# One sweep for the output projection, a gate product by token halves, and a down projection by weight rows

## The chip, the core and the metric

The kernel runs on one core of a Trainium2 chip. The metric is the device time of one execution in microseconds (us); a kernel's time is the median of several runs. TensorE (PE) multiplies, VectorE (DVE), ScalarE (ACT) and GpSimd (POOL) work element by element, SyncE (SP) issues most transfers. Each engine takes its own instructions in order and waits on semaphores. TensorE writes its sums into PSUM, of which the program uses eight banks of 128 x 512 float32.

## What is computed

A layer with two token mixers between two SwiGLU networks, for 1024 + 32 new tokens and 16 leading ones, 1024 channels wide, 2816 hidden channels, in float32:

```python
x = x + 0.5 * swiglu(rmsnorm(x, norm_ffn1), ...)
... # S5 scan on u, mLSTM on xm and z
mixed = concatenate([rmsnorm(y5, out_norm_s5), rmsnorm(ym, out_norm_ml)], axis=-1)
x = x + mixed @ w_out
x = x + 0.5 * swiglu(rmsnorm(x, norm_ffn2), ffn2_gate, ffn2_up, ffn2_down)
y = rmsnorm(x, norm_final)

def swiglu(x, w_gate, w_up, w_down):
    return (jax.nn.silu(x @ w_gate) * (x @ w_up)) @ w_down
```

The change touches the S5 half of `mixed @ w_out` and all that follows it.

## The kernel before

Channels lie on the 128 partitions, tokens along the free axis: x is eight tiles of 128 channels x 1056 tokens. For float32 accuracy each operand of a matmul is split into a high and a low part: ACT copies the value into the high part (`wh`, `vh`, `xh`, `hh`), DVE subtracts it from the value for the low part (`wl`, `vl`, `xl`, `hl`), and each product is three matmuls (high·high, high·low, low·high). `wslot` (L136) loads a 128 x 1024 slice of weights into one of two raw buffers `wr`, and splits it; `unit` makes the 24 matmuls of one output tile (L161). `psg` and `psm` hand out PSUM banks, four each.

**Output projection, S5 half.** Two sweeps over the tokens, half c=0, then c=1 (528 each). A sweep goes over the eight output tiles o in the order 0, 4, 1, 5, 2, 6, 3, 7, and loads and splits its weights anew. For each o two quarters of 264 tokens are multiplied, DVE scales them by the S5 norm `Rb` out of PSUM (L1168), DVE or, for every second o, POOL adds x (L1169), the result goes to DRAM (`x_d`) and, with the gain of the second FFN's norm, back to x. Squares for that norm are made by ACT and summed by DVE and by POOL (L1152). Once o and o-4 are there, the operands of the next stage are made: `sums` forms differences on POOL (L1291), `split` their high and low parts (ACT L1309, DVE L1310).

**Gate and up.** Two hidden tiles f, f+1 at a time, by a Strassen–Winograd scheme (class `Strassen`): seven products A·B of 512 x 256 weights with 512 x 264 tokens in place of eight. `weights` (L1317) forms the seven weight operands, `gemm` (L1352) the products (L1365), the seven token operands B11, B21, T1, T2, B22, T3, T4 stand in SBUF for each half c. For c=1 and T4 they lie in the tiles `xn` of the S5 branch, which the output projection reads. The first pair is done for c=0 (gate, up), then for c=1 with its weights loaded and split again; seven middle pairs interleave both halves; the last two pairs are again done by halves. `rms_half` (L234) makes the norm's factors for one half: the sum over channels by six one-column matmuls (`col`, L244), a reciprocal root in Newton steps on DVE (`rsqrt`, L251 to L257), and `rms_row`, which spreads it over the partitions by matmuls (`R`, L230). The gate goes through the norm, SiLU and the norm again (`silu`), is multiplied with up (`mul`) and written to DRAM as `h_d`.

**Down.** Three token blocks of 288, 384 and 384. `h_load` reads all 22 hidden tiles of a block and splits them, the first block's during the last gate products; then each output o goes through 22 x 3 matmuls into one bank (L395), with three weight slots for each o, and DVE adds the sum to x (L397). x itself comes back from `x_d` by transfers on POOL's queue (`x_back`, L1200) in two parts, since its space holds raw weights until then.

**Final norm.** `Prep` squares, sums and spreads as above; `out` multiplies the rows of a block (POOL L1223 and L1224, DVE L1226) and stores them (L1231). Blocks 0 and 1 are multiplied and stored later, during the following block; the last one is all that stands behind the last matmul.

`later()` and `behind(es)` place instructions, for engines that are not TensorE, behind what has been issued so far in the program; a scheduler sets the rest of the order.

Of the kernel before, what the change touches and what calls it, by code (L numbers as in the profile page):

```python
# [9 lines left out]
F32 = mybir.dt.float32  # L10
# [18 lines left out]
TAIL = (288, 384, 384)  # L29
# [61 lines left out]
class Kern:  # L91
# [141 lines left out]

    def rms_half(self, R, c, W, a, b):  # L234

        nc = self.nc
        c0 = list(range(0, W - P, P)) + [W - P]
        n = len(c0)
        m, y, t = (self.tp.tile([P, 2 * n], F32, tag=tag + "s", name=tag, bufs=1) for tag in ("rm", "ry", "rt"))
        col = self.psm("col")  # L240
        nc.gpsimd.tensor_tensor(a, a, b, op=ALU.add)
        for i in range(2 * n):
            s = W * (i // n) + c0[i % n]
            nc.tensor.matmul(col[:, i:i + 1], lhsT=a[:, s:s + P], rhs=self.ones, start=True, stop=True)  # L244
# [91 lines left out]
    def gate_up(self, st, wg, wu, R, pool, rest, tail):  # L336

# [3 lines left out]
        W = st.W  # L341
        both = [(f, (0, 1)) for f in range(2, NF - 4, 2)]
        ends = [(f, (c,)) for c in range(2) for f in (NF - 4, NF - 2)]
        for f, cs in [(0, (0,)), (0, (1,))] + both + ends:
            if True:
                sil = {(n, c, q): pool.tile([P, W], F32, tag=f"sil{n}{c}{q}", name="sil") for c in cs for q in range(2) for n in range(2)}

                def silu(n, c, q, src):
                    g, r = sil[n, c, q], R[:, (2 * c + q) * W:(2 * c + q + 1) * W]
                    nc.vector.tensor_tensor(g, src, r, op=ALU.mult)  # L350
                    nc.scalar.activation(g, g, AF.Silu)  # L351
                    nc.gpsimd.tensor_tensor(g, g, r, op=ALU.mult)  # L352

                def mul(n, c, q, src):
                    h = sil[n, c, q]
                    nc.vector.tensor_tensor(h, src, h, op=ALU.mult)
                    t0 = (2 * c + q) * W
                    nc.sync.dma_start(self.h_d[f + n, :, t0:t0 + W], h)
# [4 lines left out]
                st.gemm(wu[f], wu[f + 1], cs, lambda n, c, q: pool.tile([P, W], F32, tag=f"u{q}{n * q}{c}", name="u"), mul)  # L363
                if f == 0 and cs == (0,):
                    with self.later():
                        rest()
                if f == NF - 2 and cs == (0,):
                    tail()

    def h_load(self, pool, t0, n, raws):  # L370

        nc, hs = self.nc, []
        for f in range(NF):
            hh, hl = (pool.tile([P, n], F32R, tag=f"{t}{f}", name=t) for t in ("hh", "hl"))
            raw = raws(f)
            nc.sync.dma_start(raw, self.h_d[f, :, t0:t0 + n])
            nc.scalar.activation(hh, raw, AF.Copy)
            nc.vector.tensor_tensor(hl, raw, hh.bitcast(F32), op=ALU.subtract)
            hs.append((hh, hl))
        return hs  # L380

    def down(self, x, wd, pool, load, raws, post):

        nc = self.nc
        for j, (t0, n) in enumerate(post.blks):
            hs = load(j)
            for o in range(8):
                ps = self.psg()
                for i, (f, nf) in enumerate(((0, 8), (8, 7), (15, 7))):
                    w = self.wslot(wd[o, :, f * P:(f + nf) * P], nf * P, pool if i == 1 else None, 1, raws() if j == 0 else None)  # L390
                    for k in range(nf):
                        wh, wl = (t[:, k * P:(k + 1) * P] for t in w)
                        hh, hl = hs[f + k]
                        for m, (l, r) in enumerate(((wh, hh), (wh, hl), (wl, hh))):
                            nc.tensor.matmul(ps[:, :n], lhsT=l, rhs=r, start=f + k + m == 0, stop=f + k == NF - 1 and m == 2)  # L395
                xs = x[o][:, t0:t0 + n]
                nc.vector.scalar_tensor_tensor(xs, ps[:, :n], 0.5, xs, op0=ALU.mult, op1=ALU.add)  # L397
                post.sq(j, o)
            post.fin(j)
# [541 lines left out]
    def run(self):  # L941
# [193 lines left out]
        h0, esg = ExitStack(), ExitStack()  # L1135
# [442 lines left out]
```

## Time and profile before

| | us |
|---|---|
| median of 3 runs | 2499.73 (2498.15 to 2500.45) |
| the profiled execution's own time | 2500.77 |
| its span in the profile | 2499.1 |
| S5 half of the output projection and first products | 1619.1 to 1769.3 |
| gate and up | 1769.3 to 2140.6 |
| last products, down's first block and into its second | 2140.6 to 2308 |
| rest of the down projection | 2308 to 2480 |
| behind the last matmul | 2480 to 2499.1 |

The profile shows one execution; its times are microseconds from the span's start. The stretches are cut by hand, so that TensorE is busy without a gap in two of them, from 1769.3 to 2140.6 and from 2308 to 2480. A busy share of TensorE says nothing of how fast it runs: for that the profile has the granted clock (PEclk), 1.00 being the full 2.4 GHz.

### The profile page before, as it was taken

How to read it: one execution, taken by the hardware profiler on the slowest of the kernel's cores; microseconds unless marked ns; L12 is line 12 of the kernel's file. 1: busy time of each engine (PE TensorE's matmuls, PEld its weight loads, DVE VectorE, ACT ScalarE, POOL GpSimd, SP SyncE). 2: the span in 40 equal slices, each digit the busy share in tenths (PEclk: the TensorE clock that was granted, in tenths of full speed). 3: DMA queues.
4: the chain of work that ended last, by engine and by line, in shares of the span. 5: the costliest groups of instructions: out<-in, count | busy, mean ns of one | idle time of the engine just before them, and what ended most of it. 6: DMA issues, size and time to landing. Idle time of an engine off the chain costs nothing.

```text
span 2499.1 us, 41152 instructions
## 1 busy us (share of the span) xinstructions
PE 2390.3 (96%) x15656; PEld 2321.0 (93%) x15656; DVE 1491.0 (60%) x2901; ACT 883.6 (35%) x1604; POOL 1031.8 (41%) x1828
## 2 busy tenths in 40 slices
PE   8999999999999999999998989998999999889997
PEld 7999999999999978978898989997999999889997
DVE  7446444444344755537878696687765656966543
ACT  5112211111111433234544316655434344545431
POOL 3004787787787322012235170255544343430001
PEclk9999999999999999999999999998999999999998
DMA  4111222232223323332165452142222222457543
GB/s 152 55 52 55 74 76 82 75 107 82 68 76 95 134 61 68 118 106 80 41 204 178 158 161 106 43 148 91 90 88 89 82 74 86 142 182 237 165 144 111
DMA packets 171309, 264.66 MB, mean 106 GB/s; under 512 B 38704, under 2 KB 113472, under 8 KB 171112
## 3 DMA queue, kind: packets, MB, share of 16 engines
q1 hardware_dynamic: 152456, 230.33, 29.9%
q0 software_dynamic: 9808, 27.32, 3.2%
q10 hardware_dynamic: 8848, 4.38, 0.6%
q8 instruction: 123, 2.02, 0.3%
q14 instruction: 74, 0.61, 0.1%
HBM read 203.44 MB, written 62.72 MB: 107 GB/s over the span
## 4 chain that ended last, share of the span: by engine, by line
PE 64%; POOL 12%; DVE 11%; DMA 5%; issue 4%; ACT 3%; SPq 1%; POOLq 0%; ACTq 0%; DVEq 0%
PE psg L161 33%; PE psg L1365 16%; PE psg L395 8%; POOL E L495 3%; POOL et L495 2%; DMA win_d<-wi 2%; DMA hr<-h_d 1%; PE nu L868 1%; POOL wo L495 1%; PE cps L900 1%; POOL lb L495 1%; PE vp L714 1%; DVE A L629 1%; DVE xl L197 1%; DVE wl L154 1%
## 5 line engine op out<-in xcount | busy, mean ns | idle before, releaser
L161 PE MATMUL psg<-xh,wh 128*128 128x358 f32 (+4 forms) x2272 | 429.2, 328 | 9.4 <-ACT xh L196 8.5
L161 PE MATMUL psg<-xl,wh 128*128 128x358 f32 (+4 forms) x2272 | 424.3, 326 | 0.0
L161 PE MATMUL psg<-xh,wl 128*128 128x358 f32 (+4 forms) x2272 | 419.5, 324 | 0.0
L161 PEld LDWEIGHTS psg<-xh,wh 128*128 128x128 f32 x2272 | 372.9, 191 | 19.6 <-ACT xh L196 10.5
L161 PEld LDWEIGHTS psg<-xl,wh 128*128 128x128 f32 x2272 | 374.1, 191 | 5.0 <-issue 4.4
L161 PEld LDWEIGHTS psg<-xh,wl 128*128 128x128 f32 x2272 | 371.4, 190 | 3.8 <-issue 3.3
L153 ACT ACTIVATE wh<-wr 128x1024 fp32r<-128x1024 f32 (+1 forms) x170 | 176.4, 1037 | 403.2 <-PE psg L161 247.3
L154 DVE TENSOR_TENSOR wl<-wr,wh 128x1024 fp32r<-128x1024 f32 (+1 forms) x170 | 211.7, 1245 | 93.1 <-ACT wh L153 82.2
L314 DVE SCALAR_TENSOR_TENSOR x<-psg,x 128x358 f32<-128x358 f32 (+1 forms) x264 | 137.8, 527 | 100.1 <-PE psg L161 99.5
L395 PE MATMUL psg<-hh,wh 128*128 128x384 f32 (+1 forms) x528 | 171.5, 325 | 3.6 <-ACT wh L153 3.6
L395 PE MATMUL psg<-hh,wl 128*128 128x384 f32 (+1 forms) x528 | 171.1, 324 | 2.2 <-DVE wl L154 2.2
L395 PE MATMUL psg<-hl,wh 128*128 128x384 f32 (+1 forms) x528 | 170.4, 323 | 0.0
L161 PE MATMUL psg<-hh,wh 128*128 128x358 f32 (+1 forms) x528 | 133.4, 333 | 1.0 <-DVE x L314 1.0
L352 POOL TENSOR_TENSOR sil<-sil,Ra 128x264 f32<-128x264 f32 x88 | 85.1, 978 | 117.8 <-ACT sil L351 117.8
L161 PE MATMUL psg<-hl,wh 128*128 128x358 f32 (+1 forms) x528 | 131.9, 328 | 0.0
L161 PE MATMUL psg<-hh,wl 128*128 128x358 f32 (+1 forms) x528 | 129.5, 326 | 0.0
L273 DVE TENSOR_TENSOR gt<-psg,Ra 128x358 f32<-128x358 f32 (+1 forms) x66 | 34.8, 529 | 127.7 <-PE psg L161 120.9
L282 DVE TENSOR_TENSOR hf<-sil,psg 128x358 f32<-128x358 f32 (+1 forms) x66 | 34.8, 527 | 124.8 <-PE psg L161 124.8
L1435 POOL TENSOR_TENSOR acc<-acc,sq 128x358 f32<-128x358 f32 (+2 forms) x36 | 38.8, 1077 | 170.0 <-ACT sq L1433 169.3
L395 PEld LDWEIGHTS psg<-hh,wh 128*128 128x128 f32 x528 | 99.2, 188 | 4.8 <-ACT wh L153 4.8
L395 PEld LDWEIGHTS psg<-hh,wl 128*128 128x128 f32 x528 | 99.1, 188 | 2.9 <-DVE wl L154 2.9
L495 POOL TENSOR_TENSOR E<-E,et 128x8 f32<-128x8 f32 (+6 forms) x256 | 97.7, 382 | 3.8
(398 smaller groups left out, 4923.1 us busy)
## 6 DMA issues: line engine op xcount, KB each, us to landing
x<-w2g SPq DMA_DIRECT2D x28, 512.0 KB
x<-w2u SPq DMA_DIRECT2D x28, 512.0 KB
wr<-w2d SPq DMA_DIRECT2D x32, 448.0 KB
wr<-win SPq DMA_DIRECT2D x24, 512.0 KB
wr<-wout SPq DMA_DIRECT2D x24, 512.0 KB
h_d<-sil SPq DMA_DIRECT2D x88, 132.0 KB
wr<-w1g SPq DMA_DIRECT2D x22, 512.0 KB
wr<-w1u SPq DMA_DIRECT2D x22, 512.0 KB
```

What stands on the lines that cost most here:

```text
L153: nc.scalar.activation(vh, r, AF.Copy)
L154: nc.vector.tensor_tensor(vl, r, vh.bitcast(F32), op=ALU.subtract)
L161: self.nc.tensor.matmul(ps[:, :n], lhsT=a[k], rhs=b[k], start=i == 0, stop=i == 3 * nk - 1)
L197: nc.vector.scalar_tensor_tensor(l, s, gain, h.bitcast(F32), op0=ALU.mult, op1=ALU.subtract)
L273: nc.vector.tensor_tensor(gt[:, :n], ps[:, :n], R[:, t0:t0 + n], op=ALU.mult)
L282: nc.vector.tensor_tensor(hf[:, :n], sil[:, :n], ps[:, :n], op=ALU.mult)
L314: nc.vector.scalar_tensor_tensor(xs, ps[:, :n], 0.5, xs, op0=ALU.mult, op1=ALU.add)
L352: nc.gpsimd.tensor_tensor(g, g, r, op=ALU.mult)
L395: nc.tensor.matmul(ps[:, :n], lhsT=l, rhs=r, start=f + k + m == 0, stop=f + k == NF - 1 and m == 2)
L495: PT = lambda o, x, y, op: nc.gpsimd.tensor_tensor(o, x, y, op=op)
L1365: nc.tensor.matmul(ps[c, bank], lhsT=l[:, k * P:(k + 1) * P], rhs=r[k], start=start and i == k == 0, stop=i == 2 and k == 3, skip_group_ch ...
L1435: e.tensor_tensor(d, d, sq, op=ALU.add)
```

## The change

1. The S5 half of the output projection is a single sweep: each weight is loaded and split once and used for four token quarters; the first two output tiles go together. Additions of x and of squares are all DVE's. `early(k)` makes the token operands of c=0 within the sweep; `late(1)` makes the 28 splits and 16 differences of c=1 behind it (L1287 is the split's DVE line now), with `behind(es, 20)`.
2. The first pair's gate product runs all seven steps for c=0 and then for c=1; `rms_quarters` makes the norm's factors of all four quarters between the two, and their rows `R` are spread within the steps of c=1. All eleven pairs do both halves, each weight loaded once.
3. Down has blocks of 360, 360 and 336 tokens. The first two go by hidden tiles f: one row of the weights (`w2f`, 128 x 1024) and one tile of h are loaded and split, and 24 matmuls of 360 columns add to eight banks, one for each output. The third block goes by outputs as before; its h is read during the second block. x comes back in two transfers on POOL's queue behind the last up product. Rows and stores of each block follow its own norm.

The diff's core:

```diff
-        for f, cs in [(0, (0,)), (0, (1,))] + both + ends:
+        us = self.wp.tile([P, 1024], F32, tag="wr", name="u")
+        for f in range(0, NF, 2):
...
-                st.gemm(wg[f], wg[f + 1], cs, lambda n, c, q: sil[n, c, q], silu)
-                if f == 0 and cs == (0,):
-                    st.late(1)
+            st.gemm(wg[f], wg[f + 1], lambda n, c, q: sil[n, c, q], silu, rest if f == 0 else None)
+            st.gemm(wu[f], wu[f + 1], u, mul)
...
+        for j in range(last):
+            t0, n = blks[j]
+            ps = [(self.psg if o % 2 == 0 else self.psm)("psd") for o in range(8)]
+            for f in range(NF):
+                hh, hl = self.h_load(self.hp, f, t0, n, wide, bufs=4)
+                w = self.wslot(wf[f])
+                if j == last - 1:
+                    hs.append(self.h_load(pool(), f, *blks[last], wide, tag=str(f)))
+                for l, rs in zip(w, ((hh, hl), (hh,))):
+                    for o in range(8):
+                        for i, r in enumerate(rs):
+                            nc.tensor.matmul(ps[o][:, :n], lhsT=l[:, o * P:(o + 1) * P], rhs=r, start=f == i == 0 and l is w[0], stop=f == NF - 1 and l is w[1])
             for o in range(8):
...
+                add(j, o, ps[o])
...
             for c in range(2):
...
+            st.early(0)
+            for i, o in enumerate(order[2:], 2):
+                w = load(o)
+                for c in range(2):
+                    ot = new()
+                    for q in (2 * c, 2 * c + 1):
+                        evict(ot, self.unit(w, xn, W2 * q, W2), q)
+                    done(i, o, c, ot)
+                    if c == 0 and i % 2:
+                        st.early(i // 2)
...
         w = self.weights((src1, src2))
-        ps, u = {}, {}
+        if rest is not None:
+            with ExitStack() as es:
+                K.behind(es, 20)
+                self.late(1)
...
+        for i in range(7):
+            step(i, 0)
+        rows = rest()
+        for i in range(7):
+            step(i, 1)
+            if i == 0:
+                rows()
+                for h in held:
+                    out(*h)
```

Up to the output projection the two programs have the same instructions in the same order. Three places behind it follow, each as it stands before and after.

DVE, the reciprocal root of the norm. Before, the second half's (`rm`, `ry`, `rt`) stands in the middle of the first up product for c=1, and its steps come one behind another:

```order
L356 TENSOR_TENSOR sil<-psg,sil 128x264
L1334 TENSOR_TENSOR vl<-Rb,vh 128x512
L245 TENSOR_SCALAR rm<-col 128x6
L253 TENSOR_SCALAR ry<-rm 128x6
L255 TENSOR_TENSOR rt<-ry 128x6
L256 SCALAR_TENSOR_TENSOR rt<-rt,rm 128x6
L257 SCALAR_TENSOR_TENSOR ry<-rt,ry 128x6
```

After, the root of all four quarters (its tiles lie in x) stands among the last of the 28 splits of c=1 (`xl`); L347 is the first use of the factors:

```order
L257 SCALAR_TENSOR_TENSOR x<-x 128x12
L255 TENSOR_TENSOR x<-x 128x12
L1287 TENSOR_TENSOR xl_112<-x,xh_111 128x264
L256 SCALAR_TENSOR_TENSOR x<-x 128x12
L257 SCALAR_TENSOR_TENSOR x<-x 128x12
L1287 TENSOR_TENSOR xl_114<-x,xh_113 128x264
L255 TENSOR_TENSOR x<-x 128x12
L256 SCALAR_TENSOR_TENSOR x<-x 128x12
L1287 TENSOR_TENSOR xl_114<-x,xh_113 128x264
L257 SCALAR_TENSOR_TENSOR x<-x 128x12
L347 TENSOR_TENSOR sil<-sil,Ra 128x264
```

All 28 splits of c=1 now stand ahead of the root's last step (the last L257), the last five of them among the root's steps; before, no split stood between the column's sum and the root.

TensorE, the rows `R` that carry the root to all partitions. Before, they stand right behind `col`, in the middle of the up product for c=1:

```order
L1365 MATMUL psg<-xl_102,vh 128x264 x2
L1365 MATMUL psg<-xh_99,vl 128x264 x2
L1365 MATMUL psg<-xh_101,vl 128x264 x2
L244 MATMUL col<-ones,Ra 128x1 x6
L230 MATMUL R<-ident,ry 128x128 x2
L230 MATMUL R<-ident,ry 128x8
L230 MATMUL R<-ident,ry 128x128 x2
L230 MATMUL R<-ident,ry 128x8
L1365 MATMUL psg<-xh_103,wh 128x264 x2
```

After, three of four stand behind two steps of c=1 (twelve matmuls on B11, twelve on T1), and behind them the rest of the gate product:

```order
L1376 MATMUL psg<-xl_104,vh 128x264 x2
L1376 MATMUL psg<-xl_106,vh 128x264 x2
L1376 MATMUL psg<-xh_103,vl 128x264 x2
L1376 MATMUL psg<-xh_105,vl 128x264 x2
L230 MATMUL R<-ident,x 128x128 x2
L230 MATMUL R<-ident,x 128x8
L230 MATMUL R<-ident,x 128x128 x2
L230 MATMUL R<-ident,x 128x8
L230 MATMUL R<-ident,x 128x128 x2
L230 MATMUL R<-ident,x 128x8
L1376 MATMUL psg<-xh_107,wh 128x264 x2
L1376 MATMUL psg<-xh_109,wh 128x264 x2
```

The splits that the steps of c=1 read (`xh`, `xl`) and the root that `R` reads are made by the same DVE stretch.

SP, from gate and up to down. Before, h's first block is read and weights for down are issued between the last writes of h; `x<-w2d` are raw weights that lie in x's space:

```order
L1324 DMA x<-w2g 128x2x512
L358 DMA h_d<-sil 128x264
L376 DMA x<-h_d 128x288 x2
L358 DMA h_d<-sil 128x264
L376 DMA x<-h_d 128x288 x6
L358 DMA h_d<-sil 128x264
L1324 DMA x<-w2g 128x2x512
L376 DMA x<-h_d 128x288 x6
L152 DMA x<-w2d 128x2x512
```

After, one row of weights goes ahead of the last six writes of h, and reads of h and rows of weights take turns:

```order
L355 DMA h_d<-sil 128x264 x8
L152 DMA wr<-w2f 128x1024
L355 DMA h_d<-sil 128x264 x3
L369 DMA hr<-h_d 128x360 x3
L355 DMA h_d<-sil 128x264 x3
L152 DMA wr<-w2f 128x1024
L369 DMA hr<-h_d 128x360
L152 DMA wr<-w2f 128x1024
L369 DMA hr<-h_d 128x360 x3
L152 DMA wr<-w2f 128x1024
L369 DMA hr<-h_d 128x360 x2
```

The reads of h for the first block moved behind nearly all of its writes, and the weights for down go through the two buffers `wr`.

## Rows read from the trace of the kernel before

**Rows 1.** The page's first line.

```profile
span 2499.1 us, 41152 instructions
```

**Rows 2.** Windows, all engines: window, length, busy of each engine, PEclk, DMA share, GB/s.

```profile
1619.10:1769.30 150.20, 131.09 (x988) 129.74 (x987) 123.74 (x209) 77.72 (x143) 78.91 (x70) 0.90 0.37 119
1769.30:2140.60 371.30, 371.30 (x3038) 371.18 (x3039) 233.06 (x351) 156.17 (x316) 171.10 (x147) 0.99 0.26 84
2140.60:2308.00 167.40, 151.69 (x1117) 147.75 (x1116) 121.17 (x186) 87.08 (x158) 40.55 (x33) 0.99 0.62 193
2308.00:2480.00 172.00, 172.00 (x984) 172.00 (x982) 71.62 (x94) 58.69 (x79) 8.95 (x7) 1.00 0.47 140
2480.00:2499.10 19.10, 6.29 (x41) 5.69 (x41) 7.46 (x23) 2.12 (x4) 6.72 (x7) 0.58 0.46 165
```

**Rows 3.** Windows, PE by line: L161, then L1365, then L395.

```profile
1619.10:1769.30 150.20, 95.28 (x746) 0.90 0.37 119
...
1619.10:1769.30 150.20, 27.65 (x169) 0.90 0.37 119
...
2140.60:2308.00 167.40, 64.54 (x492) 0.99 0.62 193
...
2140.60:2308.00 167.40, 87.49 (x613) 0.99 0.62 193
2308.00:2480.00 172.00, 171.56 (x972) 1.00 0.47 140
```

**Rows 4.** Waits of PE, 1619.1 to 2308: total us, times, longest.

```profile
PE psg L1365 <- ACT vh L1333: 13.2, 3, 9.2
...
PE R L230 <- DVE ry L257: 2.4, 1, 2.4
```

**Rows 5.** DVE groups by shape, 1619.1 to 1769.3: busy, mean ns, idle; then POOL's L1291.

```profile
L1310 DVE TENSOR_TENSOR xl<-x,xh 128x264 fp32r<-128x264 f32 x32 | 21.3, 694 | 5.4 <-ACT xh L1309 5.3
...
L1168 DVE TENSOR_TENSOR ot<-psg,Rb 128x264 f32<-128x264 f32 x32 | 13.6, 425 | 5.4 <-PE psg L161 2.7 <-issue 1.5 <-ACT Rb L231 1.0
...
L1310 DVE TENSOR_TENSOR B22l<-x,B22h 128x264 fp32r<-128x264 f32 x4 | 3.9, 980 | 0.0
...
L1291 POOL TENSOR_TENSOR x<-x x32: 735/761/1184, 1637.9 to 1737.3; 128x264 f32<-128x264 f32 x32
```

**Rows 6.** PE's timeline around 2179.57: start, duration, count, idle before.

```profile
2174.84 0.65 PE L1365 MATMUL psg<-xh,wl 128*128 128x264 f32 x4
2179.57 1.25 PE L1365 MATMUL psg<-xh,vh 128*128 128x264 f32 x4 [4.08 <-ACT sil L1370]
```

**Rows 7.** Groups by shape, 2308 to 2480.

```profile
L154 DVE TENSOR_TENSOR wl<-wr,wh 128x1024 fp32r<-128x1024 f32 x14 | 17.8, 1270 | 34.2 <-ACT wh L153 34.2
...
L378 DVE TENSOR_TENSOR hl<-hr,hh 128x384 fp32r<-128x384 f32 x15 | 8.6, 595 | 11.7 <-ACT hh L377 11.6
L397 DVE SCALAR_TENSOR_TENSOR x<-psg,x 128x384 f32<-128x384 f32 x14 | 7.8, 556 | 17.6 <-PE psg L395 17.6
```

**Rows 8.** ACT's timeline, 2342 to 2349; landing of x_d; a window.

```profile
2342.37 0.96 ACT L153 ACTIVATE wh<-wr 128x896 fp32r<-128x896 f32 x1 [1.09 <-DMA wr<-w2d]
...
2345.95 1.06 ACT L153 ACTIVATE wh<-wr 128x1024 fp32r<-128x1024 f32 x1 [1.57 <-DMA wr<-w2d]
...
DMA to landing us min/median/max: 4.3/5.6/10.4
...
2220.00:2308.00 88.00, 84.95 (x607) 83.20 (x606) 52.19 (x86) 43.16 (x69) 2.29 (x3) 1.00 0.74 232
```

**Rows 9.** Timelines of DVE, POOL and SP at the end.

```profile
2482.81 0.60 DVE L216 TENSOR_SCALAR rm<-col 128x1 f32<-128x1 f32 x3 [2.24 <-PE col L214]
...
2485.22 0.16 DVE L257 SCALAR_TENSOR_TENSOR ry<-rt,ry 128x3 f32<-128x3 f32 x1
...
2485.24 6.72 POOL L1224 TENSOR_TENSOR x<-x,Rb 128x384 f32<-128x384 f32 x7 [48.91 <-ACT Rb L231]
...
2487.23 5.14 SPq L1231 DMA_DIRECT2D o_y<-x  x4
```

More of the change, by code (lines that the diff above doesn't have):

```diff
@@ L333, in ffn, with gate_up @@
                 pass
-    def gate_up(self, st, wg, wu, R, pool, rest, tail):
+    def gate_up(self, st, wg, wu, R, pool, rest):
         nc = self.nc
         self.h_d = self.tc.dram_tile([NF, P, TO], F32, name="h_d")
-        W = st.W
-        both = [(f, (0, 1)) for f in range(2, NF - 4, 2)]
-        ends = [(f, (c,)) for c in range(2) for f in (NF - 4, NF - 2)]
-        for f, cs in [(0, (0,)), (0, (1,))] + both + ends:
[L345 to L358, printed above, removed]
-                st.gemm(wg[f], wg[f + 1], cs, lambda n, c, q: sil[n, c, q], silu)
-                if f == 0 and cs == (0,):
-                    st.late(1)
[L363 to L382, printed above, removed]
-        nc = self.nc
-        for j, (t0, n) in enumerate(post.blks):
-            hs = load(j)
-            for o in range(8):
[L388 to L399, printed above, removed]
@@ new lines, in run, with second @@
+            st.early(0)
[3 more added lines that the diff above has]
+                    ot = new()
+                    for q in (2 * c, 2 * c + 1):
+                        evict(ot, self.unit(w, xn, W2 * q, W2), q)
+                    done(i, o, c, ot)
+                    if c == 0 and i % 2:
+                        st.early(i // 2)
+        gu = esg.enter_context(tc.tile_pool(name="gu", bufs=1, reuse_waits="tile"))
+        def rest():
+            with self.later():
+                rows = self.rms_quarters(Ra, W2)
+            def second():
+                with self.later():
+                    rows()
+            return second
@@ L1202, in run @@
[L1202 to L1217 removed]
+                nc.gpsimd.dma_start(xa[:, k:k + 4, :TO], x_d[k:k + 4].rearrange("k p t -> p k t"))
@@ L1382, in gemm, with emit @@
-        for c in cs:
-            add(nc.vector, u[c, 2], mm(c, "d", "S4", "B22", start=False), u[c, 2])
-            out(0, c, 1, u[c, 2])
-        for c in cs:
-            keep(c, 3, mm(c, "a", "S3", "T3", start=False), new(1, c, 0))
-            add(nc.gpsimd, u[c, 5], u[c, 3], u[c, 5])
-            out(1, c, 1, u[c, 5])
-        for c in cs:
-            out(1, c, 0, mm(c, "a", "A22", "T4", start=False))
+        def emit(n, c, q, t):
+            if rest is not None and c == 0:
+                held.append((n, c, q, t))
+            else:
+                out(n, c, q, t)
@@ new lines, in gemm, with __init__, tile @@
+        if rest is None:
+            for i in range(7):
+                for c in range(2):
+                    step(i, c)
+            return
+        for i in range(7):
+            step(i, 0)
+        rows = rest()
+        for i in range(7):
+            step(i, 1)
+            if i == 0:
+                rows()
+                for h in held:
+                    out(*h)
+class _Spare:
+    ROWS = {"rm": (0,), "ry": (1, 2), "rt": (3,), "rms": (4,), "rys": (5,), "rts": (6,)}
+    def __init__(self, x):
+        self.x, self.i = x, {}
+    def tile(self, shape, dt, tag=None, name=None, bufs=1):
+        r = self.ROWS[tag]
+        i = self.i[tag] = self.i.get(tag, -1) + 1
+        return self.x[:, r[i % len(r)], :shape[1]]
```

314 lines of the change are left out of this document (170 added, 144 removed).

## The prediction

> **What bounds the kernel now.** I cut the span into windows by what TensorE does and divide matmul time by instruction, since the change leaves the number of matmul columns as it is: only the gaps between matmuls can change. The span is 2499.1 us [rows 1], the execution's own time 2500.77, 1.04 above the median of 2499.73; my sum of gains is taken off the median.
>
> From 1769.3 to 2140.6 TensorE never stops: 3038 matmuls of 264 columns in 371.30 us, 0.1222 us each [rows 2]. From 2308 to 2480 it doesn't stop either: 972 of 384 columns take 171.56 us, 0.1765 each [rows 3]. Both are 0.46 ns a column, so a matmul of 360 columns is estimated at 0.1655 us, one of 288 at 0.1328, and the order in which columns are grouped is worth nothing. What can be won lies in three places.
>
> A, 1619.1 to 1769.3 (150.2 us): 746 + 169 matmuls of 264 columns [rows 3] are worth 915 x 0.1222 = 111.8 us. The rest, 38.4 us, is gaps, a clock of 0.90 [rows 2] and the 73 other small matmuls; about 5 us of these small ones (my choice; the norm needs them in any order) stays, so **33 us** are losses. The list of waits shows the largest: 13.2 us on the weight split `vh`, 9.2 in one piece [rows 4].
>
> B, 2140.6 to 2308 (167.4 us): 492 x 0.1222 + 528 x 0.1328 (down's first block) + 85 x 0.1765 = 145.2 us, so **22 us** are losses.
>
> C, behind the last matmul: **19.1 us** [rows 2].
>
> **The change, part by part.**
>
> *Single sweep.* Eight weight loads and splits go; DVE takes over POOL's additions. DVE then has, by the mean durations of [rows 5] and [rows 7], 32 evictions at 0.425, 16 additions and 14 sums of squares of 528 columns at twice that, 26 splits at 0.694 and eight weight splits at 1.27: 13.6 + 13.6 + 11.9 + 18.0 + 10.2 = 67 us in a sweep of 94 us (768 x 0.1222). TensorE's matmuls hide it but for about 2 us (0 to 6) where evictions come late: four of the eight banks serve the sweep, so DVE may lag by some three units of 2.9 us before TensorE waits.
>
> *First gate product.* Time 0 is TensorE's start on it. c=0 takes 84 x 0.1222 = 10.3 us, `col` about 1, the two steps of c=1 ahead of `R` 2.9: TensorE comes to `R` at about 14. `R` waits for the root's last step, which DVE's order has behind all 28 splits. DVE comes to the first split at about 6 (my estimate: two evictions, an addition and squares, and two weight splits are still ahead of it). How long do 28 splits take while POOL makes 16 differences? Undisturbed, a 264-column instruction is 0.425 us (L1168, whose source is PSUM [rows 5]): 11.9 us. The 32 measured `xl` splits beside POOL's differences have a mean of 0.694 [rows 5]: 19.4. If DVE and POOL took strict turns, 11.9 + 16 x 0.761 = 24.1. I take the measured 19.4. The root itself is 2.6 us (2482.81 to 2485.38 [rows 9]). So `R` is ready at 6 + 19.4 + 2.6 = 28, the wait 14 (7 to 19). A wait of 4.08 us let the next four matmuls take 1.25 in place of 0.65 us [rows 6] for some 3 us, so the clock adds about 2: 16 (9 to 21). Behind it the up product starts with its evictions in arrears: 1 (0 to 3). A' = 2 + 16 + 1 = **19** (9 to 30) in place of 33: gain 14.
>
> At this place the Trainium skill, "SBUF — State Buffer", § Who interferes with whom, has a rule against the change: a DVE instruction with two SBUF inputs and a GpSimd instruction that reads SBUF lock each other out for a whole instruction, while one with a single SBUF input goes free. The trace agrees in kind: L1168 (one operand in PSUM) stays at 0.425 while `B22l` takes 0.980, about one split plus half to all of a difference. By the strict rule the splits take the 24.1 us above, A' is 24 and the time about 5 us later than by the row.
>
> *From up to down.* h's first tile can be read when it is written, so what stands between the last up matmul and down is the first splits: `hh` and `hl` of one tile, 0.53 + 0.595 [rows 7] = 1.2 us. One raw weight buffer stays occupied by `u` until the last product: 1. The two reads of x (4.3 MB) run beside the first hidden tiles; reads of a part of it landed in 4.3 to 10.4 us [rows 8], and 232 GB/s was moved with TensorE nearly full in 2220 to 2308 [rows 8]: 1.5 (0 to 4).
>
> *Down by rows.* For each f there are 24 matmuls, 24 x 0.1655 = 3.97 us, and DVE splits 1.27 + 0.56, ACT 1.06 + 0.53: hidden. The second block reads 512 KB of weights and 2 x 172 KB of h in 3.97 us, about 220 GB/s, near the 232 above: 1.5 (0 to 4). Between the blocks all eight banks have to be evicted: 8 x 0.52 (0.556 [rows 7] by 360/384) = 4.2 us; the first bank is finished 1.2 us before the last, and the next block asks for a bank each 0.33 us, for the last at 2.3: 0.7 without and 1.9 with all overlap lost, I take 1.4. Into the third block 0.3. B' = 1.2 + 1 + 1.5 + 1.5 + 1.4 + 0.3 = **7** (2 to 14) in place of 22: gain 15.
>
> *Tail.* POOL's seven rows, 0.96 us each, ended at 2491.96 [rows 9]; four belong to block 1 and now go earlier. `Rb` stays 7.6 behind the last matmul, three rows of 336 columns (0.84) end at 10.2, the last store is issued 0.4 later and the span ended 6.7 after that issue: 17.3, gain **2** (0 to 4).
>
> Sum: 14 + 15 + 2 = 31, and 2499.7 - 31 = **2469 us**.
>
> **Rivals.**
>
> R1, the first gate product waits as long as all that is saved ahead of it. DVE and POOL take strict turns, and the wait is followed by a late up product: A' stays at 33. For it: `R` stands behind every split, and the measured `B22l` of 0.980; against: the mean of 0.694. Time 2499.7 - 17 = 2483.
>
> R2, slower: the raw weight buffers of down. There are two, and a buffer's round is the load's landing L, ACT's copy 1.06, DVE's split 1.27 and about 0.3 of issue; two buffers serve f's of 3.97 us if L + 2.6 is at most 7.9, so L up to 5.3. Before, two copies that both waited for a transfer started 3.58 us apart (2342.37, 2345.95 [rows 8]); two buffers make a round of 7.2 and L about 4.5, while h was read as well. That speaks against it, narrowly; for it speaks that x, h and weights now come together, and that x's own reads took up to 10.4. Each microsecond of L above 5.3 costs half a microsecond for each of 44 f's, 22 us; from L = 6.7 on the gain of 31 is gone, at L = 8 the time is 2528.
>
> R3, TensorE loses its clock while it goes round eight banks. The Trainium skill, "TensorE: Matmul & The Clock Gate", § A second HAM failure mode: psum-queue depth-cycling, tells of a kernel whose clock swung when it cycled banks in each iteration. As a mechanism of this kernel: at half clock the two blocks' 1056 matmuls take 175 us more, 2644. Against it: in 1769.3 to 2140.6 products change banks every twelve matmuls at a clock of 0.99, and no gap is to be seen [rows 2].
>
> R4, all is hidden: splits undisturbed at 11.9 (A' at 9) and B' at 2: gains of 24 + 20 + 4, about 2452.
>
> **How the numbers follow.** Forecast (2457 to 2480) 0.66; R1 0.15; R4 0.10; R2 0.07, of which 0.02 ends within no change; R3 0.02. The likeliest gives 2469. The range 2450 to 2492 takes in the forecast, R1, most of R4 and the mildest of R2, and leaves out about 0.13. A change under 0.2% (5 us) can't be told from none. Faster by more is the forecast, R1 and R4, less 0.01 for mishaps that add up: 0.90; within 0.03; slower 0.07.
>
> **What would show it.** Sweep: TensorE gaps from its start to the first gate matmul under 6 us in all. First gate: one wait of `R` on the root's last `ry` of about 14 us (7 to 19), splits of 0.6 to 0.8 on the mean, PEclk below 1 behind it; a mean near 0.42 speaks for R4, near 0.85 for R1. Up to down: TensorE idle 2 to 4 us. Down: 24 matmuls each 4 us at PEclk 1.00, ACT's copies waiting for TensorE rather than for transfers; waits of TensorE on `wh` or `wl` that come back every f are R2, a PEclk near 0.5 is R3. Tail: 17 us. I am wrong if the losses of A don't lie in the doubled weights and sweeps but in something that the single sweep keeps, or if the first gate's steps wait for something ahead of `R`.

## The result and the profile after

The changed kernel takes **2453.51 us** (median of four runs, 2450.63 to 2458.17) beside 2499.38 on the same chip: ratio 0.9818, 95% interval 0.9801 to 0.9835, 45.9 us less. Measured twice more beside other runs of the kernel before it had 0.9817 (0.9795 to 0.9838) and 0.9810 (0.9796 to 0.9823). The profiled execution took 2452.73, its span is 2451.0 us, 48.1 shorter than [rows 1].

Not all of the 48.1 us belongs to the change. The first row here is TensorE's row `R` ahead of the S5 half of the output projection, the second the `col` of the last norm, right behind the last matmul; both of the kernel before (start, duration, line, idle time before):

```profile
1617.55 1.56 PE L230 MATMUL R<-ident,ry 128*128 128x128 f32 x6 [3.81 <-DVE ry L257]
...
2479.82 3.40 PE L214 MATMUL col<-ones,sqd 128*128 128x1 f32 x30
```

and the same `R` after:

```profile
1613.80 1.43 PE L230 MATMUL R<-ident,ry 128*128 128x128 f32 x6 [3.82 <-DVE ry L257]
```

In front of it the two programs are alike, and yet it starts 3.75 us earlier; in the profiles of this study it starts anywhere from 1608 to 1618 us, whichever kernel it is, so this is no effect of the change (its cause was not looked for). I therefore compare stretches from here on. From this row to the last `col` (2434.97, below) it is 821.2 us in place of 862.3: **41.1 less**; behind it 16.0 in place of 19.3: **3.3 less**.

Windows of the changed kernel, all engines (columns as in [rows 2]): the sweep, the first gate product and into its up product, the rest of gate and up, down's three blocks:

```profile
1615.50:1710.30 94.80, 94.00 (x769) 93.82 (x769) 68.37 (x139) 47.53 (x92) 18.03 (x20) 0.99 0.27 88
1710.30:1757.00 46.70, 40.52 (x290) 39.04 (x289) 39.29 (x71) 25.46 (x63) 26.35 (x29) 0.85 0.19 63
1757.00:2176.00 419.00, 419.00 (x3456) 419.00 (x3455) 251.70 (x391) 170.12 (x348) 187.14 (x164) 1.00 0.27 87
2176.00:2265.00 89.00, 88.27 (x538) 88.06 (x537) 42.22 (x57) 38.60 (x55) 0.03 (x1) 1.00 0.62 207
2265.00:2355.00 90.00, 90.00 (x551) 90.00 (x550) 54.75 (x82) 47.03 (x73) 0.00 (x0) 1.00 0.61 199
2355.00:2435.00 80.00, 80.00 (x529) 80.00 (x527) 39.09 (x65) 29.36 (x40) 12.81 (x11) 1.00 0.51 157
```

From 1757 to 2435 TensorE is busy without a gap but for one at 2176, at a clock of 1.00; the losses of 2140.6 to 2308 in [rows 2] have gone. The sweep is 94.80 us for 768 matmuls whose bare time is 93.8. What is left ahead of the last matmul lies in the second window, at a clock of 0.85. TensorE's waits, from 1600 to the end (total, times, longest; the first row is left out, the two waits at a norm's root that lie outside the change, 3.8 at the `R` shown above and 2.3 behind the last matmul):

```profile
...
PE psg L1376 <- ACT sil L1381: 4.9, 3, 3.0
PE R L230 <- DVE x L257: 2.0, 2, 1.2
PE psd L398 <- ACT hh L370: 0.7, 1, 0.7
```

The 13.2 on `vh` of [rows 4] have no successor. TensorE in the first pair (start, duration, idle before):

```profile
1710.32 0.65 PE L1376 MATMUL psg<-B11h,wh 128*128 128x264 f32 x4
...
1720.83 1.25 PE L1376 MATMUL psg<-T3h,wh 128*128 128x264 f32 x4 [2.96 <-ACT sil L1381]
...
1733.54 1.25 PE L1376 MATMUL psg<-xh,vh 128*128 128x264 f32 x4 [1.47 <-ACT sil L1381]
...
1738.21 2.15 PE L230 MATMUL R<-ident,x 128*128 128x128 f32 x18 [1.24 <-DVE x L257]
```

DVE in the same stretch:

```profile
1717.12 8.62 DVE L1287 TENSOR_TENSOR xl<-x,xh 128x264 fp32r<-128x264 f32 x12
...
1726.01 8.83 DVE L1287 TENSOR_TENSOR xl<-x,xh 128x264 fp32r<-128x264 f32 x11
...
1737.90 0.16 DVE L257 SCALAR_TENSOR_TENSOR x<-x 128x12 f32<-128x12 f32 x1
```

DVE comes to the first split of c=1 6.8 us behind TensorE's start (1717.12 - 1710.32), has made 28 of them when the root's last step starts at 1737.90, and `R` starts 27.9 us behind the product's start. The steps on the way wait now and then for ACT's copies out of PSUM (`sil`), which stand in ACT's queue behind the copies for the splits.

Between up and down, and behind the last matmul:

```profile
2177.14 1.60 PE L398 MATMUL psd<-hh,wh 128*128 128x360 f32 x8 [0.73 <-ACT hh L370]
```

```profile
2434.97 3.40 PE L214 MATMUL col<-ones,sqd 128*128 128x1 f32 x30
...
2442.79 2.60 POOL L1232 TENSOR_TENSOR x<-x,Rb 128x336 f32<-128x336 f32 x3 [45.40 <-ACT Rb L231]
...
2444.56 1.25 SPq L1239 DMA_DIRECT2D o_y<-x  x2
```

One wait of 0.73 us for the first tile of h; and three rows on POOL in place of the seven of [rows 9]. ACT's copies in down (waits from 2176 to 2435) wait for TensorE far more often than for a row of weights:

```profile
ACT wh L153 <- PE psd L398: 45.5, 29, 2.9
...
ACT wh L153 <- DMA wr<-w2f: 5.2, 2, 3.6
```

### The profile page after: what moved, and what is told of

It reads as the page before. It is cut to its first block, busy times and chain, and to the rows that moved or that the text cites. A ratio compares the mean times of both kernels' runs of the same rounds, so it can differ in the third digit from the quotient of the medians.

```text
span 2451.0 us, 40952 instructions
## 1 busy us (share of the span) xinstructions
PE 2372.5 (97%) x15656; PEld 2307.7 (94%) x15656; DVE 1436.2 (59%) x2858; ACT 861.4 (35%) x1576; POOL 972.5 (40%) x1790
## 4 chain that ended last, share of the span: by engine, by line
PE 68%; POOL 11%; DVE 9%; DMA 5%; issue 4%; ACT 2%; SPq 1%; POOLq 0%; ACTq 0%; DVEq 0%
PE psg L161 35%; PE psg L1376 18%; PE psd L398 7%; POOL E L511 3%; POOL et L511 2%; DMA win_d<-wi 1%; PE psg L410 1%; DVE xl L197 1%; PE cps L916 1%; DMA rb<-rb_d 1%; PE nu L884 1%; POOL wo L511 1%; PE vp L730 1%; POOL lb L511 1%; DVE xl L1287 1%
## 5 line engine op out<-in xcount | busy, mean ns | idle before, releaser
L161 PE MATMUL psg<-xh,wh 128*128 128x358 f32 (+4 forms) x2272 | 428.0, 327 | 8.7 <-ACT xh L196 7.9
L161 PE MATMUL psg<-xl,wh 128*128 128x358 f32 (+4 forms) x2272 | 421.8, 325 | 0.0
L161 PE MATMUL psg<-xh,wl 128*128 128x358 f32 (+4 forms) x2272 | 419.2, 324 | 0.0
L161 PEld LDWEIGHTS psg<-xh,wh 128*128 128x128 f32 x2272 | 371.4, 190 | 18.9 <-ACT xh L196 9.7
L161 PEld LDWEIGHTS psg<-xl,wh 128*128 128x128 f32 x2272 | 371.8, 190 | 4.9 <-issue 4.4
L161 PEld LDWEIGHTS psg<-xh,wl 128*128 128x128 f32 x2272 | 371.1, 189 | 3.7 <-issue 3.3
L153 ACT ACTIVATE wh<-wr 128x1024 fp32r<-128x1024 f32 (+1 forms) x182 | 190.9, 1049 | 401.8 <-PE psg L161 266.7
L154 DVE TENSOR_TENSOR wl<-wr,wh 128x1024 fp32r<-128x1024 f32 (+1 forms) x182 | 229.1, 1259 | 121.3 <-ACT wh L153 84.0
L161 PE MATMUL psg<-hh,wh 128*128 128x358 f32 (+1 forms) x528 | 133.7, 334 | 0.9 <-DVE x L314 0.9
L161 PE MATMUL psg<-hl,wh 128*128 128x358 f32 (+1 forms) x528 | 132.1, 329 | 0.0
L161 PE MATMUL psg<-hh,wl 128*128 128x358 f32 (+1 forms) x528 | 129.9, 327 | 0.0
L349 POOL TENSOR_TENSOR sil<-sil,Ra 128x264 f32<-128x264 f32 x88 | 79.1, 914 | 120.6 <-ACT sil L348 120.5
L398 PE MATMUL psd<-hh,wh 128*128 128x360 f32 x352 | 113.8, 327 | 0.7 <-ACT hh L370 0.7
L398 PE MATMUL psd<-hl,wh 128*128 128x360 f32 x352 | 113.8, 327 | 0.0
L1232 POOL TENSOR_TENSOR x<-x,Rb 128x360 f32<-128x360 f32 (+1 forms) x11 | 10.9, 1018 | 245.4 <-ACT Rb L231 245.4
L511 POOL TENSOR_TENSOR et<-E 128x8 f32<-128x8 f32 (+6 forms) x256 | 92.8, 362 | 19.1
L161 PEld LDWEIGHTS psg<-hh,wh 128*128 128x128 f32 x528 | 92.5, 190 | 2.5 <-DVE x L314 2.3
L161 PEld LDWEIGHTS psg<-hl,wh 128*128 128x128 f32 x528 | 94.3, 190 | 0.0
```

Source lines behind the costliest of these rows:

```text
L153: nc.scalar.activation(vh, r, AF.Copy)
L154: nc.vector.tensor_tensor(vl, r, vh.bitcast(F32), op=ALU.subtract)
L161: self.nc.tensor.matmul(ps[:, :n], lhsT=a[k], rhs=b[k], start=i == 0, stop=i == 3 * nk - 1)
L398: nc.tensor.matmul(ps[o][:, :n], lhsT=l[:, o * P:(o + 1) * P], rhs=r, start=f == i == 0 and l is w[0], stop=f == NF - 1 and l is w[1])
L511: PT = lambda o, x, y, op: nc.gpsimd.tensor_tensor(o, x, y, op=op)
```

## The experiments

Twelve runs; times are medians beside the kernel before on the same chip.

| run | us | ratio (95%) |
|---|---|---|
| down alone | 2469.33 | 0.9891 (0.9876 to 0.9905) |
| before, additions on DVE | 2489.95 | 0.9980 (0.9969 to 0.9990) |
| before, POOL out of the sweeps | 2484.26 | 0.9945 (0.9925 to 0.9964) |
| changed, two sweeps | 2453.50 | 0.9823 (0.9808 to 0.9839) |
| changed, one raw buffer | 2540.10 | 1.0176 (1.0157 to 1.0195) |
| changed, weights read twice | 2464.48 | 0.9857 (0.9839 to 0.9876) |
| changed, low parts twice | 2461.18 | 0.9870 (0.9835 to 0.9906) |
| changed, differences on DVE | 2447.35 | 0.9802 (0.9773 to 0.9831) |
| the same again | 2445.87 | 0.9786 (0.9772 to 0.9799) |
| the same, `col` earlier | 2452.87 | 0.9806 (0.9786 to 0.9827) |
| changed, again | 2451.42 | 0.9817 (0.9795 to 0.9838) |
| changed, again | 2452.45 | 0.9810 (0.9796 to 0.9823) |

**How the gain divides.** The kernel before takes over the third part and, of the second, the undivided last two pairs; its two sweeps and its first pair by halves stay:

```diff
-TAIL = (288, 384, 384)
+TAIL = (360, 360, 336)
...
-        both = [(f, (0, 1)) for f in range(2, NF - 4, 2)]
-        ends = [(f, (c,)) for c in range(2) for f in (NF - 4, NF - 2)]
-        for f, cs in [(0, (0,)), (0, (1,))] + both + ends:
+        both = [(f, (0, 1)) for f in range(2, NF, 2)]
+        for f, cs in [(0, (0,)), (0, (1,))] + both:
```

and `h_load`, `down`, `x_back` and `out` as in the change.

> The kernel before with the third part of the change alone: all pairs behind the first interleaved, down by weight rows, x back at once, rows behind each norm; two sweeps and the first pair by halves stay. Theory, the gains of the stages are independent: the stretch from the last products to the last matmul loses some 2 us in place of 22 and the tail 3 less, so 2499.4 - 23 = about 2476 (2472 to 2481). Rival, the gain hangs on the first two parts (for instance because the first products' backlog runs on): less than 10 us, 2490 or more.

Measured: 2469.33, 26 us less than the kernel before. Its `R` and its last `col`, and its largest waits:

```profile
1613.28 1.57 PE L230 MATMUL R<-ident,ry 128*128 128x128 f32 x6 [3.79 <-DVE ry L257]
...
2451.66 3.40 PE L214 MATMUL col<-ones,sqd 128*128 128x1 f32 x30
```

```profile
PE psg L1349 <- ACT vh L1317: 9.2, 1, 9.2
```

From `R` to `col` 838.4 us: 23.9 of the 41.1 come from this part, and by difference 17.2 (838.4 - 821.2) from the sweep and the first pair. This holds to about 1 us: 1.2 of the 23.9 lie ahead of the first pair's `R`, where this program is still the kernel before (from that `R` to the last `col` it is 2451.66 - 1761.16 = 690.5 us in place of 2479.82 - 1766.60 = 713.2, so 22.7 less). The wait of 9.2 us on `vh` of the kernel before stands as it was. The theory of independent stages holds, and this part is larger than the 23 forecast.

**What the sweep's single pass is worth.** The changed kernel's sweep goes over the outputs twice, by halves, with sixteen weight loads:

```diff
-            w = [load(o) for o in order[:2]]
             for c in range(2):
+                w = [load(o) for o in order[:2]]
...
-            st.early(0)
-            for i, o in enumerate(order[2:], 2):
-                w = load(o)
-                for c in range(2):
+                if c == 0:
+                    st.early(0)
+                for i, o in enumerate(order[2:], 2):
+                    w = load(o)
```

> The changed kernel with its sweep cut in two by token halves again: sixteen weight loads and splits in place of eight, all else as changed. Theory, the weights lie under the matmuls and the stage's gain comes from where the splits of c=1 and POOL's work went: within 4 us of the changed kernel's 2453.5 (2450 to 2458), the stretch of the output projection 95 to 97 us. Rival, the halved weight traffic is what the sweep gains: 10 us or more slower, 2463 and up.

Measured: 2453.50, the same. The first gate product starts at 1709.72 behind an `R` at 1613.01, 96.7 us, after the change 96.5 (1710.32 - 1613.80). Halving the weight loads is worth nothing here: what the first part gains comes from where other work went.

**What was lost there before.** In the kernel before, the wait of 9.2 us on `vh` [rows 4] begins on POOL and DVE; POOL, then DVE, then ACT around it:

```profile
1724.01 5.19 POOL L1169 TENSOR_TENSOR ot<-x,ot 128x264 f32<-128x264 f32 x1 [3.31 <-DVE ot L1168]
```

```profile
1723.85 1.79 DVE L1310 TENSOR_TENSOR xl<-x,xh 128x264 fp32r<-128x264 f32 x5
1725.57 1.21 DVE L1334 TENSOR_TENSOR wl<-x,wh 128x1024 fp32r<-128x1024 f32 x1
1726.70 0.76 DVE L1310 TENSOR_TENSOR xl<-x,xh 128x264 fp32r<-128x264 f32 x2
1727.39 1.21 DVE L1334 TENSOR_TENSOR wl<-x,wh 128x1024 fp32r<-128x1024 f32 x1
1730.85 5.36 DVE L1310 TENSOR_TENSOR xl<-x,xh 128x264 fp32r<-128x264 f32 x4 [2.24 <-ACT xh L1309]
```

```profile
1729.23 0.73 ACT L1171 ACTIVATE x<-ot,vec 128x528 f32<-128x528 f32 x1 [4.64 <-POOL ot L1169]
...
1731.66 0.61 ACT L1333 ACTIVATE vh<-x 128x512 fp32r<-128x512 f32 x1
```

One addition of 264 columns takes 5.19 us on POOL (a difference of that size has a median of 0.761 [rows 5]) while DVE runs seven splits and two weight splits with no pause, up to 1728.60; it ends at 1729.20, 0.6 us after they do. ACT waits 4.64 us for it, and `vh` stands in ACT's queue behind that. The first run takes the additions off POOL:

```diff
-                        (nc.gpsimd if i % 2 else nc.vector).tensor_tensor(t, x[o][:, t0:t0 + n], t, op=ALU.add)
+                        nc.vector.tensor_tensor(t, x[o][:, t0:t0 + n], t, op=ALU.add)
...
-                    e, d = (nc.gpsimd, accs[c][1]) if i % 2 else (nc.vector, accs[c][0])
+                    e, d = nc.vector, accs[c][i % 2]
```

> The kernel before with all additions of its two sweeps (x, and the squares) on DVE, none on POOL: a piece of the first part alone. Theory, POOL's slow additions and their fight with DVE make the backlog that TensorE waits 9.2 us for at the first gate product: 8 us or more gained, 2491 or less. Rival, the backlog is DVE's and ACT's own splits in the middle of the sweeps: DVE, busy 124 of 150 us there, takes 14 us more, and the time stays within 5 us of 2499 or grows.

Measured: 5.4 us gained by the medians, 5.0 by the ratio; the theory's 8 did not come, and the rival's number is met or just missed. POOL and TensorE there:

```profile
1714.85 4.51 POOL L1291 TENSOR_TENSOR x<-x 128x264 f32<-128x264 f32 x1 [5.28 <-DVE xl L1310]
...
1724.94 1.25 PE L1365 MATMUL psg<-T1h,vh 128*128 128x264 f32 x4 [11.14 <-ACT vh L1333]
```

The wait has not gone but moved: now a difference (L1291) is starved for 4.51 us behind the same dense run. The second run takes the differences off POOL as well:

```diff
-        sub = lambda o, x, y: self.K.nc.gpsimd.tensor_tensor(o, x, y, op=ALU.subtract)
+        sub = lambda o, x, y: self.K.nc.vector.tensor_tensor(o, x, y, op=ALU.subtract)
```

> As the last but the differences of the token operands too are DVE's: POOL has nothing left of the kernel before's two sweeps but the sums of weights. In the run before this one the wait of TensorE at the first gate product stayed (11.1 us), now behind one difference on POOL that took 4.51 us while DVE ran splits and sums back to back, as an addition had taken 5.19 in the kernel before. Theory, POOL is starved there by DVE's dense run and ACT, TensorE stand behind it: the wait on the split vh falls to 3 us or less and 10 us or more are gained on the kernel before. Rival, DVE's total load sets the wait: 32 more instructions of 0.42 us on it, the wait stays at 9 or grows, and the time is that of the last run (5 us gained) or worse.

Measured: 15 us less than the kernel before by the medians, 13.7 by the ratio.

```profile
PE psg L1365 <- ACT vh L1333: 7.3, 1, 7.3
```

```profile
1713.95 0.73 ACT L1171 ACTIVATE x<-ot,vec 128x528 f32<-128x528 f32 x1 [2.05 <-DVE ot L1169]
...
1717.52 0.42 ACT L1309 ACTIVATE xh<-x 128x264 fp32r<-128x264 f32 x1 [1.37 <-DVE x L1291]
```

The gain is the theory's, the wait is not: 7.3 us, not 3. Now ACT waits for an addition and for a difference in DVE's own queue, behind those splits, and makes `vh` right behind the second (the second block). So starvation costs part of the wait; that the order of DVE's and ACT's queues at the end of the sweep is all of the rest is read from these rows, and no run tried another order. In the changed kernel the splits of c=1 stand behind the weight operands of the first product, and no wait on `vh` is left in its list.

**What limits the first gate product now.** Each of the 28 low parts of c=1 is computed twice:

```diff
+                h, l = self.B[1, n][k]
+                self.K.nc.vector.tensor_tensor(l, {"B11": b11, "B21": b21, "T1": b11, "T2": b11, "B22": b22, "T3": b12, "T4": b21}[n], h.bitcast(F32), op=ALU.subtract)
```

> The changed kernel with each of the 28 low parts of late(1) computed twice on DVE (the same values). Theory, DVE's queue ahead of the root sets when R is released and all that TensorE loses in the first pair: 28 more instructions of 0.42 to 0.75 us make R 12 to 20 us later and the kernel as much slower, 2465 to 2474. Rival, ACT's and POOL's chain sets the pace and DVE has slack in it: under 6 us slower.

```profile
1705.65 0.65 PE L1378 MATMUL psg<-B11h,wh 128*128 128x264 f32 x4
...
1745.58 2.08 PE L230 MATMUL R<-ident,x 128*128 128x128 f32 x18
...
2184.64 1.58 PE L398 MATMUL psd<-hh,wh 128*128 128x360 f32 x8 [1.65 <-ACT hh L370]
```

```profile
1742.61 0.17 DVE L257 SCALAR_TENSOR_TENSOR x<-x 128x12 f32<-128x12 f32 x1
```

```profile
PE psg L1378 <- ACT xh L1286: 8.8, 4, 6.1
```

`R` starts 39.9 us behind the product's start in place of 27.9, and from the product's start to down it is 479.0 in place of 466.8 (2177.14 - 1710.32): 12.2 us more. By the medians it is 9.8 us slower than the repeat beside it (2461.18 to 2451.42), under the theory's 12 to 20 and over the rival's 6. So more work on DVE does lengthen the pair, but the rival's chain takes part: the root ends 37.1 us behind the product's start (1742.61 + 0.17 - 1705.65), 9.4 later than in the changed kernel, and `R` starts 2.8 us behind that without waiting for it. TensorE is late because it waits 8.8 us at the second step of c=1 for ACT's copies `xh`; ACT waits there for POOL's differences, and POOL stood 6.2 us idle until a split of DVE's. The run doesn't show one queue that sets the pair alone. The other way round, the 16 differences go from POOL to DVE:

```diff
-                    self.sub(b11, b12, b11)
+                    self.K.nc.vector.tensor_tensor(b11, b12, b11, op=ALU.subtract)
```

(and the three other kinds alike).

> The changed kernel with the 16 differences of late(1) on DVE in place of POOL. Theory, DVE's queue sets the end of the first gate product: 28 splits and 16 differences undisturbed at 0.425 are 18.7 us against 20.8 measured for the stretch with POOL beside it, R is released 25 to 28 us behind the start of the product (27.7 measured), a split's mean falls from 0.75 to under 0.5, and the time stays within 3 us of the changed kernel. Rival, POOL's differences and the ACT copies behind them set it: R comes 5 us or more earlier and 4 us or more are gained.

> The differences on DVE once more, with more rounds, beside the changed kernel on the same chip: from the first gate product to down 464.0 us against 466.8 and 467.4 in the profiles, so 3 us faster than the changed kernel, 2448 to 2450. Rival: the three microseconds come back as waits elsewhere or the runs' own spread hides them; within 1 us.

Measured: 2447.35 and 2445.87, 4.1 and 6.6 us under the changed kernel beside each. TensorE's start and `R`, and the splits, of the second run; then the splits of the changed kernel:

```profile
1705.61 0.65 PE L1376 MATMUL psg<-B11h,wh 128*128 128x264 f32 x4
...
1731.07 2.48 PE L230 MATMUL R<-ident,x 128*128 128x128 f32 x18
...
L1287 DVE TENSOR_TENSOR xl<-x,xh 128x264 fp32r<-128x264 f32 x30 | 12.4, 450 | 0.0
```

```profile
L1287 DVE TENSOR_TENSOR xl<-x,xh 128x264 fp32r<-128x264 f32 x30 | 21.0, 754 | 0.0
```

The mean of a split falls from 0.754 to 0.450 us, `R` starts 25.5 us behind the product's start, and from the product's start to down it is 464.0 us in both profiles (2169.57 - 1705.61): 2.8 less than in the changed kernel's first profile. From the first split of c=1 to the root's end it is 17.5 us in place of 20.9. Sixteen instructions more on DVE make its stretch shorter, since they cost it less than POOL's cost it beside its splits.

The changed kernel itself is less even. Its repeat beside the first run takes 467.4 us from the product's start to down, the one beside the second 470.9 (2177.34 - 1706.47):

```profile
1706.47 0.65 PE L1376 MATMUL psg<-B11h,wh 128*128 128x264 f32 x4
...
1734.36 3.98 PE L230 MATMUL R<-ident,x 128*128 128x128 f32 x18 [1.22 <-DVE x L257]
...
2177.34 1.58 PE L398 MATMUL psd<-hh,wh 128*128 128x360 f32 x8 [2.34 <-ACT hh L370]
```

Here too `R` starts 27.9 us behind the product, but its rows run at a granted clock of 0.50 and take 3.98 us in place of 2.15, the up product starts 37.5 us behind the gate product in place of 35.0, and h's first tile is waited for 1.6 us longer. So the differences on DVE gain 2.8, 3.5 or 6.9 us in this stretch, by the profile that they are set against. Of the 13.1 us between the first two profiles 9.6 lie ahead of the change, of the 7.8 between the second two 0.9. In the second comparison the intervals of the ratios, 0.9772 to 0.9799 and 0.9796 to 0.9823, just overlap. This is the fastest version measured.

With that, `col` was put behind the fifth step of c=0:

```diff
         for i in range(7):
             step(i, 0)
-        rows = rest()
+            if i == 4:
+                rows = rest()
```

> The differences on DVE as in the run before, and the one-column matmuls of the norm (col) behind the fifth step of c=0 in place of the seventh, so that the root's sum is there earlier. Theory, the rows R then stand behind five steps of c=1 instead of two and TensorE fills the wait for DVE with them: first pair 1 to 4 us shorter than with the differences alone, so 2443 to 2448. Rival, TensorE waits for the splits of those steps instead, which DVE makes in the same stretch: within 1 us of the differences alone.

Measured: 2452.87, no gain, and 7.0 us more than the differences alone, where the rival had 1. TensorE's start, `R` and the start of down:

```profile
1708.13 0.65 PE L1376 MATMUL psg<-B11h,wh 128*128 128x264 f32 x4
...
1734.54 2.19 PE L230 MATMUL R<-ident,x 128*128 128x128 f32 x18
...
2174.85 2.59 PE L398 MATMUL psd<-hh,wh 128*128 128x360 f32 x8 [2.86 <-ACT hh L370]
```

`R` starts 26.4 us behind the product's start, later than 25.5, and the stretch to down is 466.7 us in place of 464.0. The wait of 3.0 us that the differences alone left on `sil` is gone, but the first pair's clock is 0.89 in place of 0.96 (46.7 us from the product's start), and h's first tile is waited for 2.9 us. So neither number came. Of the 6.9 us between the two profiles 2.5 lie ahead of the sweep and explain nothing.

**The rival on raw weights.** A single raw buffer in the two row-wise blocks:

```diff
-                w = self.wslot(wf[f])
+                w = self.wslot(wf[f], raw=self.hp.tile([P, 1024], F32, tag="r1", name="wr", bufs=1))
```

> The changed kernel with a single raw weight buffer in the two blocks by weight rows. The cost measures the landing time L of a row of weights: a round is L + 1.06 + 1.27 + 0.3 = L + 2.6 us and replaces the 3.93 us of a hidden tile, 44 times. With the 4.5 us that the prediction's rival on raw buffers worked out: 44 x 3.2 = 140 us slower, about 2593. With L = 2.5 (much slack): 50 us slower, about 2505. If time grows by under 15 us, the round isn't what the rival took it for.

Measured: 2540.10. ACT's copies of weights (start, duration, idle before and what ended it):

```profile
2210.22 1.06 ACT L153 ACTIVATE wh<-wr 128x1024 fp32r<-128x1024 f32 x1 [4.29 <-DMA wr<-w2f]
...
2215.92 1.06 ACT L153 ACTIVATE wh<-wr 128x1024 fp32r<-128x1024 f32 x1 [4.25 <-DMA wr<-w2f]
```

A round is 5.70 us (2215.92 - 2210.22), so L = 5.70 - 2.6 = 3.1 us, not 4.5; two buffers would bear 5.3. Most rounds of the two blocks take 5.6 to 6.0 us, and 44 times 1.77 more than 3.93 are 78 of the 87 us by which this run is slower. And every row of weights read twice:

```diff
                 w = self.wslot(wf[f])
+                nc.sync.dma_start(self.hp.tile([P, 1024], F32, tag="r2", name="extra", bufs=2), wf[f])
```

> The changed kernel with each row of weights of the two row-wise blocks read a second time into a scratch tile that nothing uses: 1.2 MB for each hidden tile of the first block and 1.4 MB in the second, that is 305 and 350 GB/s at 3.93 us each. Theory, transfers have room in these blocks (198 GB/s measured at a share of 0.6): the first block keeps its pace, the second loses a few tenths of a microsecond for each tile, 5 to 15 us in all. Rival of the prediction, the blocks stand near the bound of transfers, where it put 1.5 us of loss: 40 us or more slower.

```profile
2185.00:2260.00 75.00, 72.14 (x428) 69.68 (x427) 32.43 (x40) 28.77 (x39) 0.00 (x0) 1.00 0.99 359
```

12 us slower than the changed kernel beside it (2464.48, of two executions, to 2452.45), within the theory's bounds; but the first block pays too, which the theory had at its old pace: 359 GB/s at a share of 0.99, TensorE busy 72.14 of 75 us, where the changed kernel moved some 200 (207 in the window 2176 to 2265 above). The room was there, and it is used up at about twice the weights.

> The changed kernel once more, as the reference for the two runs above on the same chip: 2453.5 (2449 to 2458).

> The changed kernel as the reference for the two runs above: 2451 to 2454.

Both repeats gave what was expected.

## Why the prediction was right, and where its sizes were off

The direction, the places and the range of 2450 to 2492 were right. The forecast's own band, 2457 to 2480, given 0.66, was missed by 3.5 us: 2469 was 15.5 us too slow, and the time came out where R4, given 0.10, had put it. By the prediction's own steps:

- *What is lost before.* The sweep and the first pair gained 17.2 us, up to down and down 23.9 and the end 3.3, each to about 1 us, so the 33 and 22 us counted as losses are of the right size; the 22 was short by some 2 us, which were not traced.
- *Single sweep*: 2 us forecast. The one wait within it is 0.8 us, at a norm's root. But the prediction saw the losses of A "in the doubled weights and sweeps", and here its reason failed: sixteen loads cost the same as eight. What was lost stood in POOL's starved additions and differences and in the order of DVE's and ACT's queues, which the new sweep changes as well; so far the gain came by luck.
- *First gate product*: `R` ready at 28, measured 27.74 (1737.90 + 0.16 - 1710.32), by misses that cancel: DVE came to the splits at 6.8, not 6, a split's mean was 0.754, not 0.694, and the root's 2.6 us did not stand behind the splits but among the last five of them. The wait of 14 us at `R` isn't one row of 14: TensorE spends the time at earlier steps, in waits for ACT's copies `sil` (4.9 us) and at half clock (0.50 from 1719.8 to 1726.6 and from 1730.0 to 1736.8), and `R` itself waits 1.24. So in this profile the 2 us for the clock lie inside the wait, not behind it; in the repeat whose `R` took 3.98 us they stand behind it, 2.5 us. No wait of evictions in arrears, put at 1, is in the list. A' came to about 16 in place of 19 (33 less 17.2), with a gain of 17.2 for 14.
- *The step that was mis-sized most is B' = 7*. Of its six stalls one shows: 0.73 us at the first tile of h, in place of 1.2 (1.4 and 2.3 in the repeats). The raw buffer held by `u`, the reads of x, the second block's transfers, the turn of the banks and the third block have no wait in the list. The run with doubled reads shows why for the transfers: down needs about 200 GB/s and 359 can be had; the 232 beside which I put the 220 was what was asked for then, not what could be given. For the banks: eight evictions took 3.6 us (2263.25 to 2266.85 on DVE), not 4.2, and began while the last weights' low parts still ran. Each term was small and got a middle value; six middles of small ranges made 7 us, and the runs showed next to nothing in their place.
- *Tail*: 17.3 forecast, 16.0 measured. Rows and stores went as forecast; the span ended some 5 us behind the last store's issue, not 6.7.
- *R1*, the lock of DVE and POOL: the two do slow each other (0.450 to 0.754 us for a split, 5.19 for an addition), but this took part in what was lost before as well, so the gain did not vanish. *R2*: TensorE has no wait on `wh` or `wl` in down, ACT's copies waited for rows of weights twice in the 44, and L = 3.1. *R3*: the windows show a clock of 1.00 through both blocks over eight banks. The case that the Trainium skill tells of ("TensorE: Matmul & The Clock Gate", § A second HAM failure mode: psum-queue depth-cycling) did not come here; it has short pauses of TensorE between groups of matmuls, and here TensorE is busy without one but for the 0.73 us. *R4*, all hidden, 2452, was nearest to the measured time, for half of its reason: B' fell to its lower bound, A' did not.

About 3.75 us of the profiles' difference lie ahead of the change and explain nothing; the medians, 45.9 us apart, are 1.5 us more apart than the 44.4 that the stretches show.

## What to carry to other kernels

A stall estimated at a seam of a kernel should need a row that shows that resource at its limit; a rate that was merely asked for, as the 232 GB/s here, bounds nothing, and several small stalls at a time sum to a bias. Loads that lay under matmuls were worth nothing when halved: ask which queue the work behind them stands in. Where a helper engine and the busy one slow each other, moving the helper's work onto the busy one can shorten the busy one's own queue: try it where rows of one shape have two durations. And before a gain of a few microseconds is read from two profiles, take the reference more than once: the same stretch of the changed kernel took 466.8, 467.4 and 470.9 us.

## What the runs showed of the hardware

A POOL addition, whose median is 1.19 us in the kernel before and whose shortest record 0.75, took 5.19, and in another kernel a difference 4.51, while DVE ran instructions with two SBUF operands back to back; both ended 0.6 us behind the end of DVE's run. The Trainium skill ("SBUF — State Buffer", § Who interferes with whom) calls the shared port pair an exclusive lock for a whole instruction. The trace agrees that the two engines hold each other up (0.450 and 0.754 us for the same split without and with POOL). But POOL was kept out over nine DVE instructions in a row here, while in the changed kernel, where DVE has as little idle time ahead of its splits (0.0 in the row above), the two took turns:

```profile
1717.63 7.14 POOL L1281 TENSOR_TENSOR x<-x 128x264 f32<-128x264 f32 x8 [6.66 <-DVE xl L1287]
```

That is 0.89 us for a difference, beside twelve splits in 8.62 us. Which of the two happens was not settled.

A 512 KB row of weights landed about 3.1 us behind its issue in the run with one raw buffer (5.70 less copy, split and an assumed 0.3 us of issue), with reads of h beside it, and one core's transfers reached 359 GB/s over 75 us.
